# Four row buffers throughout, a later start for part of the first gather, and second products in fp32 in a two-block fp32 network on one core

## The chip, the cores and the metric

The kernel runs on one core of one Trainium2 chip. A core has five engines that run side by side and meet only through semaphores: PE multiplies matrices (PEld in the profile is its weight load), DVE does elementwise work and reductions, ACT does functions and copies with a scale, POOL (GpSimd) does elementwise work too and issues the gathers, SP issues the other transfers. Each engine works through its own list of instructions in order. The metric is the device time of one execution in microseconds (us).

## The reference, cut to what matters

Input `x` has 512 tokens of 1024 numbers, handled as four token tiles of 128. A first block mixes tokens (retention and differential attention), then each token picks 8 times 16 of 16384 single-neuron experts and adds their outputs; a second block (sparse attention, pooling, gates, projections) follows. The picked experts are what this change touches:

```python
ue = jnp.take(u, e, axis=0)      # e: 128 tokens x 8 heads x 16 picks, rows of 1024 floats
ve = jnp.take(v, e, axis=0)
act = jax.nn.gelu(jnp.einsum('thkd,td->thk', ue, xb))
return jnp.einsum('thk,thkd->td', g * act, ve)
```

Everything is float32. `u` and `v` hold 16384 rows of 4 KB, 64 MB each.

## The kernel before, in words

The experts are computed in two ways. **Token tiles 0 and 3 gather** (`gather`, `fetch`): for each of the 128 picks one indirect transfer, issued by POOL, fetches one row of `u` per token into a buffer `rows` of 128x1024 (512 KB). DVE multiplies it with the normalised token and sums (L535). Then 128 fetches from `v`, each multiplied by its weight and added into `gx` (L542). So a tile takes 256 fetches, and the two tiles 512, one tile after the other. `ROWS = 3` buffers `rows` go round: fetch k can be issued when DVE has used fetch k-3. Late in tile 3 one more buffer (`more`) is taken in turn. `issue_after(x)` keeps a fetch behind instruction x in the schedule; `HOLDS` says from which fetch of a tile this x is the end of the spread (`self.mark`, a POOL copy of the last spread column). 256 means never.

**Token tiles 1 and 2 are computed densely** over all 16384 experts, in 128 groups of 128. `up` loads 128 rows of `u` (512 KB), transposes them on PE, multiplies with the 256 tokens and takes the gelu. The first 46 ups multiply in fp32 (`xw`, `EARLY = 36` into `sa`, `WX = 10` more into `w`, "ahead"); the other 82 use three products of a split into two float32r halves (`dh`, with `uT` split by ACT and DVE, L127 and L128). `spread` writes the picks' weights to their expert columns: for 64 groups of four tokens DVE makes two one-hot tiles `E`, ACT scales one (`A`), PE multiplies, DVE multiplies `sa` with the result and DVE or ACT copies the rest into `sb`. `dense` then runs over the 128 groups: load 128 rows of `v`, and four products 128x512 into the sums (`op`, the "down"). With `MIX = (1, 2)` every second down is split: ACT and DVE make halves `h`, `l` of `v` and of the weights, in one buffer each, and PE does three products in float32r in place of one in fp32.

The order on each engine is made when the program is built: a scheduler simulates the program and lists each engine's instructions. Instructions of the gather stand among those of the mixer, of the dense part and of the second block. An engine that stands at a gather instruction whose row has not landed does nothing else.

The stages, by the trace: the mixer and the expert scores of tiles 1 to 3 with tile 0's gather beside them (to about 440 us), early ups and picks (to 724), the spread (724 to 869), the dense part (869 to 1647), the second block of tiles 0 to 2 (from 1647) and of tile 3 (after it). Tile 3's gather ends at about 1850, and its result is needed only by the last of these.

Other names: `scores` normalises a tile into `xnt` (one buffer) and transposes it; `rope_tables` makes sine and cosine tables; L128 on POOL makes the low half `wlo` of a weight.

Of the kernel before, what the change touches and what calls it, by code (L numbers as in the profile page):

```python
# [8 lines left out]
F32 = mybir.dt.float32  # L9
# [57 lines left out]
class Net:  # L67
    def __init__(self, tc, ctx, a, const_at, dbg=None):
        self.tc, self.nc, self.ctx, self.a = tc, tc.nc, ctx, a
        self.dbg = dbg or {}  # L70
        self.const_at = const_at
        nc = self.nc
        pool = lambda name, bufs=1, **k: ctx.enter_context(tc.tile_pool(name=name, bufs=bufs, **k))
        self.keep = pool("keep")
        self.wk = pool("wk", 2)
        self.ps = pool("ps", 1, space=bass.MemoryType.PSUM)
        self.dram = pool("dram", 1, space=bass.MemoryType.DRAM)
        self.ident = self.const(self.keep, "ident")
# [4 lines left out]
        nc.gpsimd.memset(self.half, -0.5)  # L83
        self.turn = 0
        self.whole = True
        self.last = None
# [338 lines left out]
    def scores(self, ts, sp, sw):  # L425

        nc, a, tc = self.nc, self.a, self.tc
        n = len(ts)
        hl = self.pair(n)
        with self.behind():  # L430
            g = self.row(sw, a["norm_ffn_g"], D, "grow", bufs=1)
        for i, t in enumerate(ts):
            xn = sw.tile([P, D], F32, name="xnt", bufs=1)
            self.norm(xn, self.xs[t], g)
            o = DENSE.index(t) * P if t in DENSE else None
            self.tsplit(hl, xn, 0, i, whole=None if o is None else self.xw[:, :, o:o + P])
            if t in GATHER:
                nc.sync.dma_start(self.xnd[t], xn)
            nc.sync.dma_start(self.xd[t], self.xs[t])
        self.normed = self.root.ins  # L440
        for t in ts:
            st = sp.tile([P, 16, P], F32, name=f"s{t}", bufs=1)
            self.s[t] = st
        for b in range(4):
            qT = sw.tile([P, 4, n * P], F32, name="pqT")
            self.projT(hl, a["peer_wq"][0], b * 512, n, qT, [1.0] * 4, sw)
            for i, t in enumerate(ts):
                p = self.sc()
                for j in range(4):
                    nc.tensor.matmul(p[:, j * P:(j + 1) * P], qT[:, j, i * P:(i + 1) * P],  # L450
                                     self.skT[:, 4 * b + j, :], start=True, stop=True)
                nc.scalar.activation(self.s[t][:, 4 * b:4 * b + 4, :].rearrange("p a b -> p (a b)"), p, AF.Copy)
        return hl

    def select(self, t, sw, idx, parts=1):
# [6 lines left out]
        if not dense:  # L462
            ei = self.ga.tile([P, P], I32, name=f"ei{t}", bufs=1)
            gws = self.ga.tile([P, 8, 16], F32, name=f"gw{t}", bufs=1)
            self.ei[t], self.gw[t] = ei, flat(gws)
# [57 lines left out]

    def gather(self, t, hold, more):


        nc, a = self.nc, self.a
        ei, gw = self.ei[t], self.gw[t]
        act = self.ga.tile([P, P], F32, name="act")
        pause = self.normed if t == 0 else None  # L530
        xn = self.ga.tile([P, D], F32, name="gx", bufs=1)
        nc.sync.dma_start(xn, self.xnd[t])
        for k in range(P):
            r = self.fetch(a["peer_u"][0], ei, k, self.mark if k >= hold else pause if k >= PAUSE else None, k >= more)
            nc.vector.scalar_tensor_tensor(r, r, 1.0, xn, op0=OP.mult, op1=OP.mult, accum_out=act[:, k:k + 1])  # L535
# [4 lines left out]
        for k in range(P):  # L540
            r = self.fetch(a["peer_v"][0], ei, k, self.mark if P + k >= hold else pause, P + k >= more)
            nc.vector.scalar_tensor_tensor(x, r, act[:, k:k + 1], x, op0=OP.mult, op1=OP.add)  # L542
# [4 lines left out]

    def fetch(self, src, ei, k, hold, more):
        if more and k % (ROWS + MORE) >= ROWS:
            r = self.gm.tile([P, D], F32, name="more", bufs=MORE)  # L550
        else:
            r = self.ga.tile([P, D], F32, name="rows", bufs=ROWS)
        with self.tc.issue_after(hold) if hold else ExitStack():
# [4 lines left out]
    def spread(self, idx, sa, sb, gb):  # L558
# [3 lines left out]
        full = [P, P, 4]  # L562
        cr = self.const(gb, "row", bufs=1)
        row4 = gb.tile(full, F16, name="row4", bufs=1)
        nc.scalar.activation(row4, cr[:, :, None].to_broadcast(full), AF.Copy)
        for t in range(0, sa.shape[2], 4):
# [50 lines left out]
    def dense(self, ts, hl, sa, sb, dn, ue):  # L617
# [13 lines left out]
        def op(e):  # L631
            v, w = [V.pop(e)], [slot(e)]
            if e % MIX[1] < MIX[0]:
                for x in (v, w):
                    hl_ = [dn.tile(list(x[0].shape), F32R, name=f"{q}{x[0].shape[1]}", bufs=1) for q in "hl"]
                    self.split(*hl_, x[0])
                    x[:] = hl_
# [33 lines left out]

    def rope_tables(self, pool):

# [18 lines left out]
        lim = 3.1415925  # L692
        sin = self.keep.tile(full, F32, name="sin")
        cos = self.keep.tile(full, F32, name="cos")
        nc.vector.tensor_scalar(sin, ang, lim, -lim, op0=OP.min, op1=OP.max)
# [266 lines left out]

ROWS = 3
RAW = 3
HALFE = 4
WX = 10
DEEP = 1
PEB = 2
P0B = 2
VB = 3  # L970
EARLY = 36
MIX = (1, 2)
LASTUP = 124
# [5 lines left out]
HOLD = 252  # L979
HOLDS = [256, 0]  # L980
MORE = 1
MORES = [256, 230]
AB = 3
# [14 lines left out]
def build(tc, a, const_at, dbg=None):  # L998
    with ExitStack() as ctx:
        n = Net(tc, ctx, a, const_at, dbg)  # L1000
        pool = lambda name, bufs=1, **k: tc.tile_pool(name=name, bufs=bufs, **k)
        n.ga = ctx.enter_context(pool("ga", 2, side="right"))
        first(n, pool)
        n.tpn, n.nraw, n.whole, n.lone, n.lo_of = GN, 3, WHOLE, False, LO3
        with pool("tp2") as n.tp, pool("hn2", 2) as n.hn, pool("ws2") as n.ws, pool("b2") as b2, \
                pool("bp") as bp, pool("gm") as n.gm, pool("bw", 2) as bw:
            for t, hold, more in zip(GATHER, HOLDS, MORES):
                n.gather(t, hold, more)
            n.second_setup(b2)
# [3 lines left out]

def first(n, pool):
    n.tpn, n.nraw = 3, 4
    n.whole, n.lone = WHOLE0, True
    nd = len(DENSE) * P
    with ExitStack() as right:
        with pool("xe") as n.xe, pool("tp1") as n.tp, pool("ws1") as n.ws, pool("sk") as sk:
            with pool("b1") as b1, pool("hn") as n.hn:  # L1020
# [10 lines left out]
                n.lo_of = LO2  # L1031
                n.mixer([1, 2, 3])
            n.st = right.enter_context(pool("st", side="right"))
            picks = right.enter_context(ExitStack())
# [56 lines left out]
```

## Time and profile before

| | us |
|---|---|
| three runs | 2151.7, 2159.73, 2160.89 |
| their median | 2159.73 |
| the profiled execution, its own time | 2150.35 |
| its span | 2148.6 |

| engine | busy us | share of the span |
|---|---|---|
| PE | 1870.3 | 87% |
| PEld | 1477.7 | 69% |
| DVE | 1487.0 | 69% |
| ACT | 743.6 | 35% |
| POOL | 822.8 | 38% |

The transfers moved 538 MB, 251 GB/s on the mean. The shares are means over stages that differ: what bounds a stage is read from the windows and waits of that stage. PE's busy time counts modelled ends, so how long a product holds PE is read from the starts of two in a row. A group of fp32 products has two PE instructions for each product of the program.

### The profile page before, as it was taken

The numbers are of one execution on the slowest core, as the hardware profiler recorded it, in microseconds if no ns is written. First come the engines' busy times: TensorE is split into PE (matmuls) and PEld (weight loads), VectorE is DVE, ScalarE is ACT, GpSimd is POOL, SyncE is SP. The second block draws the span as 40 slices with busy tenths as digits, with TensorE's granted clock in tenths as the row PEclk, the third lists the DMA queues.
The fourth block names the chain that finished last, engine by engine and source line by source line (L and its number), as shares of the span: only waits on it lengthen the run. The fifth ranks groups of instructions, "written<-read, shape, count | busy, mean of one in ns | idle before, by whom it ended". The sixth has DMA issues, their size and how long they took to land.

```text
span 2148.6 us, 27755 instructions
## 1 busy us (share of the span) xinstructions
PE 1870.3 (87%) x9646; PEld 1477.7 (69%) x9646; DVE 1487.0 (69%) x3049; ACT 743.6 (35%) x1517; POOL 822.8 (38%) x627
## 2 busy tenths in 40 slices
PE   7798987588898866799999998999996698799998
PEld 6497766488777765577677776777774576677654
DVE  1188787777995799876676666676777789934261
ACT  2243442233433467332232222232232233463231
POOL 0015455443144521443433444333335787433200
PEclk9999999699999899899999999999998789899998
DMA  8847887787458763788899888899897766422872
GB/s 314 288 153 254 274 269 245 269 280 238 145 196 285 263 201 108 249 328 313 314 364 325 312 300 310 324 326 321 316 328 256 241 202 186 132 89 79 287 255 79
DMA packets 182012, 538.23 MB, mean 251 GB/s; under 512 B 18032, under 2 KB 25328, under 8 KB 181744
## 3 DMA queue, kind: packets, MB, share of 16 engines
q0 software_dynamic: 73728, 268.47, 36.4%
q1 hardware_dynamic: 108144, 268.00, 36.0%
q8 instruction: 76, 1.25, 0.2%
q14 instruction: 64, 0.52, 0.1%
HBM read 528.53 MB, written 7.86 MB: 250 GB/s over the span
## 4 chain that ended last, share of the span: by engine, by line
PE 25%; issue 23%; DMA 22%; DVE 18%; POOL 10%; ACT 1%; SPq 0%; POOLq 0%; DVEq 0%; ACTq 0%
DMA rows<-in_peer_v,ei 14%; PE acc L204 12%; POOL rows L554 9%; DMA rows<-in_peer_u,ei 7%; PE acc L232 6%; DVE gx L542 4%; DVE rows L535 2%; PE acc L642 1%; PE tr L153 1%; DVE ix L404 1%; PE sc L924 1%; DVE E L572 1%; PE tr L933 1%; DVE v L402 1%; PE sc L604 1%
## 5 line engine op out<-in xcount | busy, mean ns | idle before, releaser
L554 POOL DMA_INDIRECT rows<-in_peer_u,ei x256 | 313.2, 1224 | 444.6 <-DVE rows L535 344.3
L554 POOL DMA_INDIRECT rows<-in_peer_v,ei x249 | 286.8, 1152 | 426.7 <-DVE gx L542 350.0
L542 DVE SCALAR_TENSOR_TENSOR gx<-rows,act,gx 128x1024 f32<-128x1024 f32 x249 | 349.4, 1403 | 133.3 <-DMA rows<-in_peer_v,ei 128.1
L535 DVE SCALAR_TENSOR_TENSOR rows<-rows,gx 128x1024 f32<-128x1024 f32 x256 | 313.0, 1230 | 181.4 <-DMA rows<-in_peer_u,ei 177.8
L604 PE MATMUL sc<-dh,uT 128*128 128x256 f32 x1968 | 306.7, 305 | 29.2 <-DVE uT L128 17.6
L604 PEld LDWEIGHTS sc<-dh,uT 128*128 128x128 f32 x1968 | 261.9, 195 | 70.0 <-issue 31.3
L204 PE MATMUL acc<-wlo,Thi 128*128 128x512 f32 (+1 forms) x504 | 206.8, 430 | 9.2 <-POOL wlo L128 8.0
L204 PE MATMUL acc<-whi,Thi 128*128 128x512 f32 (+1 forms) x500 | 196.1, 429 | 14.9 <-ACT whi L127 10.6
L604 PE MATMUL sc<-xw,uT 128*128 128x256 f32 x736 | 179.7, 396 | 31.1 <-ACT uT L156 30.1
L128 POOL TENSOR_TENSOR wlo<-raw,whi 128x1024 fp32r<-128x1024 f32 (+1 forms) x62 | 144.7, 2341 | 125.0 <-ACT whi L127 124.5
L204 PE MATMUL acc<-whi,Tlo 128*128 128x512 f32 (+1 forms) x432 | 173.3, 404 | 7.9 <-DVE Tlo L128 7.9
L604 PEld LDWEIGHTS sc<-xw,uT 128*128 128x128 f32 x736 | 141.3, 199 | 52.5 <-ACT uT L156 32.7
L642 PE MATMUL acc<-v,sb 128*128 128x512 f32 x368 | 168.3, 599 | 7.7 <-DVE sb L653 7.7
L127 ACT ACTIVATE whi<-raw 128x1024 fp32r<-128x1024 f32 (+1 forms) x108 | 110.8, 1028 | 149.8 <-PE acc L204 67.1
L605 ACT ACTIVATE w<-sc 128x256 f32<-128x256 f32 x92 | 35.3, 384 | 292.7 <-PE sc L604 290.9
L204 PEld LDWEIGHTS acc<-whi,Thi 128*128 128x128 f32 x500 | 98.8, 200 | 53.0 <-issue 17.1
L204 PEld LDWEIGHTS acc<-wlo,Thi 128*128 128x128 f32 x504 | 101.3, 201 | 45.9 <-issue 18.8
L153 PE MATMUL tr<-c_ident,raw 128*128 128x128 f32 x880 | 131.5, 278 | 1.0 <-PE acc L577 1.0
L127 ACT ACTIVATE uT<-tr 128x512 fp32r<-128x512 f32 x164 | 92.8, 595 | 95.4 <-PE tr L153 84.7
L642 PEld LDWEIGHTS acc<-v,sb 128*128 128x128 f32 x368 | 68.7, 191 | 77.3 <-issue 65.8
L642 PE MATMUL acc<-h,h 128*128 128x512 f32 x256 | 104.4, 416 | 13.3 <-ACT h L127 13.1
L128 DVE TENSOR_TENSOR uT<-tr,uT 128x512 fp32r<-128x512 f32 x164 | 108.4, 685 | 7.5 <-ACT uT L127 7.2
(328 smaller groups left out, 3404.4 us busy)
## 6 DMA issues: line engine op xcount, KB each, us to landing
raw<-in_peer_u SPq DMA_DIRECT2D x128, 512.0 KB, 6.1
v<-in_peer_v SPq DMA_DIRECT2D x128, 512.0 KB, 5.7
raw<-in_w_in SPq DMA_DIRECT2D x79, 512.0 KB, 4.5
raw<-in_w_out SPq DMA_DIRECT2D x22, 512.0 KB, 4.1
whi<-in_w_in SPq DMA_DIRECT2D x21, 512.0 KB, 6.1
raw<-in_peer_wq SPq DMA_DIRECT2D x21, 512.0 KB, 5.9
wlo<-in_w_in SPq DMA_DIRECT2D x20, 512.0 KB, 6.5
rows<-in_peer_u,ei POOLq DMA_INDIRECT x256, 6.5
```

The costliest lines, as they stand in the source:

```text
L127: self.nc.scalar.activation(hi, src, AF.Copy)
L128: (eng or self.nc.vector).tensor_tensor(lo, src, hi.bitcast(F32), OP.subtract)
L153: nc.tensor.transpose(p[:, c, :], src[:, (j + c) * P:(j + c + 1) * P], self.ident)
L204: self.nc.tensor.matmul(ps[i][:, :n], x, y, start=k == 0 and q == 0, stop=k == nk - 1 and q == len(ws) - 1)
L232: nc.tensor.matmul(ps[c][:, :ncol], x, y, start=k == 0 and q == 0, stop=k == 7 and q == len(ws) - 1)
L402: nc.vector.max(v[:, r], src)
L535: nc.vector.scalar_tensor_tensor(r, r, 1.0, xn, op0=OP.mult, op1=OP.mult, accum_out=act[:, k:k + 1])
L542: nc.vector.scalar_tensor_tensor(x, r, act[:, k:k + 1], x, op0=OP.mult, op1=OP.add)
L554: self.nc.gpsimd.indirect_dma_start(out=r, out_offset=None, in_=src, in_offset=bass.IndirectOffsetOnAxis(ap=ei[:, k:k + 1], axis=0))
L604: nc.tensor.matmul(h[:, :nt], x, y, start=f == k == q == 0, stop=f == 1 and k == 3 and q == len(ps) - 1)
L605: nc.scalar.activation(dst, h[:, :nt], AF.Gelu)
L642: mm(o[i][c], x, y, start=e == q == 0, stop=e == P - 1 and q == len(ps) - 1)
```

## The change

- **Rows.** `ROWS` is 4 in place of 3, and the extra buffer `more` is gone.
- **Hold.** `HOLDS` is [168, 0]: fetches of tile 0 from the 169th on stand behind the end of the spread.
- **Downs.** `MIX` is (0, 1): no down is split. The buffers of `v` are 4 in place of 3.
- **Spread.** Of the copies into `sb` 48 of 64 are DVE's and 16 ACT's (32 and 32 before), and its row of constants shares a buffer of `A`.
- **Smaller ones.** `EARLY` 37 and `WX` 9 in place of 36 and 10; two buffers of `xnt`; the sine and cosine tables are made after the scores of tiles 1 to 3, not before those of tile 0; the picks and `act` of the gathers live in pools of their own.

```diff
-            xn = sw.tile([P, D], F32, name="xnt", bufs=1)
+            xn = sw.tile([P, D], F32, name="xnt")
...
-            r = self.fetch(a["peer_u"][0], ei, k, self.mark if k >= hold else pause if k >= PAUSE else None, k >= more)
+            r = self.fetch(a["peer_u"][0], ei, k, self.mark if k >= hold else pause if k >= PAUSE else None)
...
-    def fetch(self, src, ei, k, hold, more):
-        if more and k % (ROWS + MORE) >= ROWS:
-            r = self.gm.tile([P, D], F32, name="more", bufs=MORE)
-        else:
-            r = self.ga.tile([P, D], F32, name="rows", bufs=ROWS)
+    def fetch(self, src, ei, k, hold):
+        r = self.ga.tile([P, D], F32, name="rows", bufs=ROWS)
...
-            if t % 8:
+            if t % 16:
                 nc.vector.tensor_copy(sb[:, :, t:t + 4], g[:, EARLY:, :])
...
-ROWS = 3
+ROWS = 4
-WX = 10
+WX = 9
-VB = 3
-EARLY = 36
-MIX = (1, 2)
+VB = 4
+EARLY = 37
+MIX = (0, 1)
-HOLDS = [256, 0]
-MORE = 1
-MORES = [256, 230]
+HOLDS = [168, 0]
...
-                with pool("rt") as rt:
-                    n.rope_tables(rt)
...
+            with pool("rt") as rt:
+                n.rope_tables(rt, g3)
```

How the instructions move. The first place is POOL's list around the end of the spread, `held`; `oh` belongs to the picks of tile 3, `in_peer_v` before it and behind it is tile 0's gather, `in_peer_u` behind that tile 3's. Before:

```order
L554 DMA rows<-in_peer_v,ei_922 128x1024 x19
L501 TENSOR_TENSOR oh<-oh,ixb 128x2048
L554 DMA rows<-in_peer_v,ei_922 128x1024 x44
L610 COPY held<-sb 128x1
L554 DMA rows<-in_peer_v,ei_922 128x1024 x43
L554 DMA rows<-in_peer_u,ei_4795 128x1024 x26
```

Now:

```order
L501 TENSOR_TENSOR oh<-oh,ixb 128x2048
L555 DMA rows<-in_peer_v,ei_82 128x1024 x8
L501 TENSOR_TENSOR oh<-oh,ixb 128x2048
L613 COPY held<-sb 128x1
L555 DMA rows<-in_peer_v,ei_82 128x1024 x88
L555 DMA rows<-in_peer_u,ei_2800 128x1024 x8
```

Before, 44 fetches stood between the last pick and `held`, and 43 of tile 0 behind it; now none stands between the two, and 88 behind `held`. Up to the point where the second block clears its tail (`MEMSET tail`), 253 fetches stood behind `held` before and 305 do now.

The second place is DVE's list in the dense part, where one up (two `uT`) takes its turn with rows of tile 3. Before:

```order
L653 TENSOR_TENSOR sb<-sb,w 128x256
L535 SCALAR_TENSOR_TENSOR rows,act<-rows,gx 128x1024 x2
L128 TENSOR_TENSOR uT<-tr,uT 128x512 x2
L128 TENSOR_TENSOR l_9344<-sb,h_9343 128x256
L128 TENSOR_TENSOR l_9340<-v,h_9339 128x1024
L535 SCALAR_TENSOR_TENSOR rows,act<-rows,gx 128x1024 x2
```

Now:

```order
L657 TENSOR_TENSOR sb<-sb,w 128x256
L539 SCALAR_TENSOR_TENSOR rows,act_2802<-rows,gx 128x1024
L129 TENSOR_TENSOR uT<-tr,uT 128x512 x2
L539 SCALAR_TENSOR_TENSOR rows,act_2802<-rows,gx 128x1024 x4
L657 TENSOR_TENSOR sb<-sb,w 128x256
```

The halves `l` of the weights and of `v` are gone, and four rows stand in each up's turn where three to four stood.

The third place is the end of tile 3's gather in DVE's list. The names around it are the second block's: `isc` with its MAX and MATCH_REPLACE picks keys, `pe,mx` is softmax, `pfirst` and `uT` pooling. Before:

```order
L542 SCALAR_TENSOR_TENSOR gx<-rows,act,gx 128x1024
L908 MATCH_REPLACE isc<-m_14115,isc 128x384
L908 MATCH_REPLACE isc<-m_14118,isc 128x256
L957 SCALAR_TENSOR_TENSOR uT<-psum__15550,uT 128x384
L371 ISA pe,mx<-sc,c_blk 128x128
L371 ISA mx 128x1
L907 MAX m_14121<-isc 128x8
L907 MAX m_14124<-isc 128x8
L959 COPY uT<-pfirst 128x16
L542 SCALAR_TENSOR_TENSOR gx<-more,act,gx 128x1024
```

Now:

```order
L905 SCALAR_TENSOR_TENSOR isc<-rl,qi,isc 128x256 x2
L546 SCALAR_TENSOR_TENSOR gx<-rows,act_2802,gx 128x1024
L906 TENSOR_TENSOR isc<-isc,c_blk 128x128
L546 SCALAR_TENSOR_TENSOR gx<-rows,act_2802,gx 128x1024
L911 MAX m_13053<-isc 128x8
L912 MATCH_REPLACE isc<-m_13053,isc 128x256
L903 TENSOR_SCALAR isc<-rl,qi 128x384
L905 SCALAR_TENSOR_TENSOR isc<-rl,qi,isc 128x384
L546 SCALAR_TENSOR_TENSOR gx<-rows,act_2802,gx 128x1024
L802 TENSOR_TENSOR qk<-qk,rstd 128x640
L546 SCALAR_TENSOR_TENSOR gx<-rows,act_2802,gx 128x1024
```

The last rows stood among the softmax and the pooling of tiles 0 to 2; now a few more follow the first MAX of the key choice, and none is left when the softmax begins.

## Rows read from the trace of the kernel before

**Rows 1.** Windows by stage: start:end us, length, each engine's busy us, PEclk, DMA share, GB/s.

```profile
440.00:724.00 284.00, 244.98 (x1312) 219.68 (x1312) 230.83 (x770) 98.05 (x170) 113.15 (x81) 0.93 0.67 227
724.00:869.00 145.00, 107.32 (x695) 94.69 (x693) 137.19 (x266) 103.24 (x313) 41.22 (x40) 0.95 0.56 179
869.00:1647.00 778.00, 725.44 (x3896) 559.39 (x3896) 542.42 (x774) 218.43 (x381) 301.38 (x256) 0.98 0.87 315
1647.00:1850.00 203.00, 143.81 (x627) 114.44 (x626) 173.96 (x237) 62.70 (x112) 146.84 (x94) 0.82 0.65 207
1850.00:2149.00 299.00, 285.38 (x1185) 191.39 (x1183) 122.05 (x298) 113.81 (x209) 68.74 (x32) 0.97 0.47 156
```

**Rows 2.** Waits of PE, 869 to 1647: waiting line, releaser, total us, times, longest.

```profile
PE sc L604 <- DVE uT L128: 17.6, 12, 3.1
PE acc L642 <- ACT h L127: 13.1, 10, 2.9
PE sc L604 <- ACT dh L127: 8.2, 1, 8.2
...
PE acc L642 <- DVE l L128: 4.3, 5, 1.1
```

**Rows 3.** Waits of DVE, 869 to 1647.

```profile
DVE rows L535 <- DMA rows<-in_peer_u,ei: 104.3, 39, 5.0
```

**Rows 4.** Windows, POOL instructions on `rows` (fetches) alone: busy us, (count), clock, DMA, GB/s.

```profile
869.00:1647.00 778.00, 296.45 (x253) 0.98 0.87 315
```

**Rows 5.** DMA issues by line, 869 to 1647: count, KB each, median us to landing.

```profile
rows<-in_peer_u,ei POOLq DMA_INDIRECT x128, 7.0
```

**Rows 6.** DMA issues by line, 790 to 868.

```profile
rows<-in_peer_v,ei POOLq DMA_INDIRECT x16, 4.3
```

**Rows 7.** DMA view, 880 to 1000: rate in 40 slices of 3 us.

```profile
GB/s 339 400 333 303 164 276 377 386 251 333 374 369 389 332 403 367 344 188 156 419 421 235 247 393 404 369 385 362 126 329 399 309 182 304 358 348 89 411 412 320
```

**Rows 8.** Waits of PE, 1647 to 1850.

```profile
PE sc L924 <- DVE mx L371: 18.3, 2, 11.2
```

**Rows 9.** Timeline of DVE, 1769 to 1850: start us, length, line, operation.

```profile
1769.85 0.43 DVE L907 MAX8 m<-isc 128x8 f32<-128x256 f32 x1
...
1848.94 1.27 DVE L542 SCALAR_TENSOR_TENSOR gx<-more,act,gx 128x1024 f32<-128x1024 f32 x1
```

**Rows 10.** Timeline of PE, 1207.6 to 1222 (merged where alike).

```profile
1207.84 0.40 PE L642 MATMUL acc<-h,l 128*128 128x512 f32 x1
...
1210.13 3.59 PE L642 MATMUL acc<-v,sb 128*128 128x512 f32 x8
...
1215.79 2.65 PE L604 MATMUL sc<-dh,uT 128*128 128x256 f32 x20 [1.60 <-DVE uT L128]
1218.28 1.04 PE L153 MATMUL tr<-c_ident,raw 128*128 128x128 f32 x8
1219.07 0.48 PE L642 MATMUL acc<-h,h 128*128 128x512 f32 x1
```

**Rows 11.** Timeline of PE's weight loads (PEld), 1213.3 to 1214.

```profile
1213.56 0.42 PEld L604 LDWEIGHTS sc<-dh,uT 128*128 128x128 f32 x3 [0.24 <-issue]
```

**Rows 12.** Windows, DVE instructions on `rows` alone, in the spread.

```profile
724.00:869.00 145.00, 51.04 (x40) 0.95 0.56 179
```

**Rows 13.** Groups of DVE instructions in the spread: count, busy us, mean ns, idle before.

```profile
L582 DVE COPY sb<-acc 128x368 f32<-128x368 f32 x32 | 17.7, 552 | 0.0
```

**Rows 14.** Groups of ACT instructions in the spread.

```profile
L584 ACT ACTIVATE sb<-acc 128x368 f32<-128x368 f32 x32 | 14.8, 462 | 19.9 <-DVE sa L580 19.8
```

**Rows 15.** Waits of PE in the spread, 724 to 869.

```profile
PE acc L577 <- DVE E L572: 21.6, 27, 1.6
```

**Rows 16.** Waits of PE, 165 to 440.

```profile
PE tr L153 <- DVE xnt L145: 22.8, 3, 12.4
```

**Rows 17.** Waits of PE, 440 to 724.

```profile
PE sc L604 <- ACT uT L156: 28.5, 7, 11.3
```

**Rows 18.** Timeline of ACT, 0 to 1: an activation table load.

```profile
0.72 1.28 ACT L255 ACT_TABLE_LOAD   x1 [0.72 <-PEq L1077]
```

More of the change, by code (lines that the diff above doesn't have):

```diff
@@ L83, in __init__ @@
         nc.gpsimd.memset(self.half, -0.5)
+        self.picks, self.act = {}, {}
         self.turn = 0
@@ L462, in select @@
         if not dense:
-            ei = self.ga.tile([P, P], I32, name=f"ei{t}", bufs=1)
-            gws = self.ga.tile([P, 8, 16], F32, name=f"gw{t}", bufs=1)
+            ei, gws = self.picks[t]
             self.ei[t], self.gw[t] = ei, flat(gws)
@@ L522, in select, with room, gather @@
             nc.scalar.activation(self.gk[:, o:o + P], p[:, 2, :], AF.Copy)
-    def gather(self, t, hold, more):
+    def room(self, t, pool):
+        self.picks[t] = pool.tile([P, P], I32, name=f"ei{t}"), pool.tile([P, 8, 16], F32, name=f"gw{t}")
+        self.act[t] = pool.tile([P, P], F32, name=f"act{t}")
+    def gather(self, t, hold):
         nc, a = self.nc, self.a
         ei, gw = self.ei[t], self.gw[t]
-        act = self.ga.tile([P, P], F32, name="act")
+        act = self.act[t]
         pause = self.normed if t == 0 else None
@@ L540, in gather @@
         for k in range(P):
-            r = self.fetch(a["peer_v"][0], ei, k, self.mark if P + k >= hold else pause, P + k >= more)
+            r = self.fetch(a["peer_v"][0], ei, k, self.mark if P + k >= hold else pause)
             nc.vector.scalar_tensor_tensor(x, r, act[:, k:k + 1], x, op0=OP.mult, op1=OP.add)
@@ L562, in spread @@
         full = [P, P, 4]
-        cr = self.const(gb, "row", bufs=1)
+        cr = gb.tile([P, 4, P], F32, name="A", bufs=AB)[:, 0, :]
+        o, _ = self.const_at["row"]
+        nc.sync.dma_start(cr, self.a["consts"][:, o:o + P])
         row4 = gb.tile(full, F16, name="row4", bufs=1)
@@ L634, in op @@
                 for x in (v, w):
-                    hl_ = [dn.tile(list(x[0].shape), F32R, name=f"{q}{x[0].shape[1]}", bufs=1) for q in "hl"]
+                    hl_ = [dn.tile(list(x[0].shape), F32R, name=f"h{x[0].shape[1]}", bufs=1),
+                           dn.tile(list(x[0].shape), F32R, name=f"l{x[0].shape[1]}", bufs=1)]
                     self.split(*hl_, x[0])
@@ L669, in after, with rope_tables @@
         return x
-    def rope_tables(self, pool):
+    def rope_tables(self, pool, keep):
         nc, a = self.nc, self.a
@@ L692, in rope_tables @@
         lim = 3.1415925
-        sin = self.keep.tile(full, F32, name="sin")
-        cos = self.keep.tile(full, F32, name="cos")
+        sin = keep.tile(full, F32, name="sin")
+        cos = keep.tile(full, F32, name="cos")
         nc.vector.tensor_scalar(sin, ang, lim, -lim, op0=OP.min, op1=OP.max)
@@ L1002, in build @@
         n.ga = ctx.enter_context(pool("ga", 2, side="right"))
-        first(n, pool)
+        n.room(0, ctx.enter_context(pool("g0", side="right")))
+        first(n, pool, ctx)
         n.tpn, n.nraw, n.whole, n.lone, n.lo_of = GN, 3, WHOLE, False, LO3
         with pool("tp2") as n.tp, pool("hn2", 2) as n.hn, pool("ws2") as n.ws, pool("b2") as b2, \
-                pool("bp") as bp, pool("gm") as n.gm, pool("bw", 2) as bw:
-            for t, hold, more in zip(GATHER, HOLDS, MORES):
-                n.gather(t, hold, more)
+                pool("bp") as bp, pool("bw", 2) as bw:
+            for t, hold in zip(GATHER, HOLDS):
+                n.gather(t, hold)
             n.second_setup(b2)
@@ L1011, in build, with first @@
                 n.second(ts, bp, bw)
-def first(n, pool):
+def first(n, pool, ctx):
     n.tpn, n.nraw = 3, 4
@@ L1032, in first @@
                 n.mixer([1, 2, 3])
+            g3 = ctx.enter_context(pool("g3", side="right"))
+            n.room(3, g3)
             n.st = right.enter_context(pool("st", side="right"))
```

## The prediction

> **What bounds the kernel now.** I read the windows by stage first, then the waits inside each stage, then the timeline where a wait needed a price. The windows [rows 1] show no single bound. In the spread (145 us) DVE works 137.2 us: DVE bounds it. In the dense part (778 us) PE works 725 us with modelled ends, and its waits [rows 2] name the other engines for little: 17.6 us on DVE's `uT`, 13.1 on ACT's `h`, 8.2 at the start on `dh`, 4.3 on `l`. DVE itself stands there 104 us waiting for `u` rows alone [rows 3], and a `uT` queued behind such a row is late. The transfers run at 315 GB/s with 253 fetches issued [rows 1, 4]: one fetch each 778/253 = 3.07 us, so with three buffers a round of 9.2 us, of which 7.0 us pass from issue to landing [rows 5]. At 109 GB/s in the spread's later part the landing takes 4.3 us [rows 6]. From 1647 to 1850 PE works only 144 of 203 us, at a mean granted clock of 0.82 between its levels of 1.2 and 2.4 GHz, with stands before it; its longest wait is 18.3 us on softmax maxima from DVE [rows 8], whose list is filled with rows until 1849 [rows 9]. After that PE works 285 of 299 us: it bounds the end, and tile 3's gather is not waited for but stands in others' way.
>
> **Early stages.** The norm of the next tile no longer waits for the last one's transposes, since `xnt` has two buffers. PE waits for `xnt` 22.8 us in three waits, the first of 12.4 [rows 16]; the first stays, the other two (10.4) mostly go: -8. One fp32 up more stands ahead of the spread. By the timeline's spacing of 0.43 us for an fp32 product of 512 columns [rows 10, 11] its 16 instructions of 256 columns take half of that each, with eight transposes of 0.10 us: 16 x 0.215 + 0.8 = 4.2, say +4. Four more table loads of 1.28 us [rows 18] come where PE already waits 28.5 us for ACT's `uT` [rows 17]: 0 to +5, taken as +4 with the 13 short DVE operations of the tables. Fetches of tile 0 come faster with four buffers; that can shorten DVE's stands or slow weight loads, which I cannot sign. Sum 0, with -25 (all the `xnt` wait and some more) and +15 (none of it, and both additions doubled) as ends.
>
> **The spread.** By 724, when it begins, about as many fetches have been issued as the new limit of 168 allows, so nothing is lost before it. Behind the held fetch POOL has only fetches, 88 of tile 0 and the first of tile 3, so the wait stops nobody else; DVE's list has their rows behind the spread too. The 40 rows inside it, 51.0 us of DVE [rows 12], go behind it. Added on DVE are 16 copies of 0.55 us less about 0.1 that overlaps, +7.2 [rows 13]: 137.2 - 51.0 + 7.2 = 93. ACT drops 16 copies of 0.46 [rows 14] and one up's evacuations (1.6): 103.2 - 7.4 - 1.6 = 94. PE drops one up: 107.3 - 5 = 102. So the stage cannot go below 102 (-43); if PE's wait of 21.6 us on `E` [rows 15] and half as much on ACT stay on top of it, it is 135 (-10). I take 110, nearer to the busiest engine since the wait on `E` was DVE being full: -35.
>
> **The dense part.** The 64 split downs become fp32. Products in float32r start 0.229 us apart (1207.84 to 1210.13, ten of them), a down has 12: 2.75 us. The fp32 down starts at 1210.13, and the load behind the first following one at 1213.56: 3.43 us for 8 [rows 10, 11]. That is +0.69 on PE, times 64 = +44. (The eight seem to end at 1213.16, but the next product's start there is followed by a gap; the weight loads show the true pace.) Going by an up of 24 x 0.1245 + 0.79 = 3.8 us [rows 10] and 82 of them, PE's floor was 176 + 220 + 310 + 10 (`dh`) = 716 of the 778; it becomes 440 + 310 + 10 = 760. The stalls were 62. The waits for `h` and `l`, 17.4, go with the splits, which leaves 45. Also gone are 64 splits of `v` and of the weights on ACT and DVE; a down then waits for the landing of `v` alone, three groups ahead with four buffers, which I cost at nothing. How much of the rest goes depends on the rows. DVE's list has 305 - 253 = 52 fetches more in this stage, and they must come at 788/305 = 2.58 us, a round of 10.3 us for four buffers against 9.2 now. That leaves 1.1 us for slower landings. The bytes: 315 GB/s x 778 = 245 MB, plus 52 x 0.524 = 272 MB, in 788 us 346 GB/s. On a line through 4.3 us at 109 GB/s and 7.0 at 315 the landing grows to 7.4, by 0.4. So rows come early enough more often than before, and I take 28 of the 45 us as staying: 788, +10. Ends: no stall, 760 (-18); all 45, 805 (+27).
>
> The Trainium skill (FP8 and Floating Point Precision, TensorE Precision Notes) counts four passes for true fp32. With the float32r spacing for each pass that would be 4 x 0.229 = 0.92 us in place of the 0.86 that the rows show, and an estimate of +59 us in place of +44; the rows decide.
>
> **The second block.** Rows left for it by the lists are 39 in place of 46, and the last one stands where the first key choice does, which ran at 1769.85; before it was at 1848.94 [rows 9]. Softmax of tiles 0 to 2 then meets no gather on DVE, nor POOL's issues between weight splits. The 18.3 us wait goes, and a little of the slow clock with it: -20. Ends: -45 (three quarters of the 59 us that PE does not work before 1850) and 0 (the rows that crowd into its first 120 us take back what the later part gives).
>
> **Sum.** 0 - 35 + 10 - 20 = -45. Against the profiled execution's 2150.35 that is 2105. The median of the three runs is 9.4 above that execution and the lowest 1.4 above; I add 3: 2108.
>
> **Rivals.** *Transfers at their limit (slower).* If the transfers cannot go past 315 GB/s, 272 MB take 865 us, the fourth row only waits longer in the queue, and rows that stand ahead of `uT` in DVE's list hold PE: dense +87 in place of +10, so 2108 + 77 = 2185. It decides from a dense part of 833 us on (no gain in all), 2.73 us for a fetch or 327 GB/s. For it: landings already take 7.0 against 4.3 us. Against it: slices of 3 us reach 421 GB/s, and 369 to 403 are common [rows 7]. The Trainium skill (DMA: Bandwidth & Descriptors, Specifications) gives a core about 358 GB/s of its memory; the slices pass that for short, and by that limit, as an estimate, 272 MB would take 761 us, and this rival would not decide.
>
> *The gains are covered (no change).* In the spread the engines wait on each other in turn (-10), in the dense part all 45 us of stalls stay (+27), and the second block gives 5: +12, so 2165. For it: each wait in [rows 2] is short and spread over several engines, as in a chain without one bound.
>
> *More than forecast.* Two rows more in hand take nearly all stalls from the dense part (-10), early stages give 12, the spread reaches its floor (-43), the second block 35: -100, so 2053. For it: DVE's list loses all splits `l`, and its stands on rows are long [rows 3].
>
> That the hold does nothing would need fetch 169 to come late anyway; the 40 rows inside the spread [rows 12] speak against it.
>
> **How the numbers follow.** The forecast has 0.64 (its own range 2075 to 2140), the larger gain 0.13, no change 0.12, the transfer limit 0.11. About 0.5% (11 us) is what a measurement of this kernel can tell: faster means below 2149, slower above 2170. Faster: 0.62 of the forecast, the larger gain 0.13 and 0.02 of no change, 0.77. Same: 0.02 and 0.07, 0.09. Slower: the transfer limit and 0.03, 0.14. The range of 8 in 10 is 2052 to 2158: it reaches to the larger gain and part of the way to no change, and leaves out the transfer limit.
>
> **What would show it.** Right: a spread of about 110 us without L542 in it, a dense part of 770 to 805 us with DVE's waits for `u` rows under the 104 us of now, some 340 GB/s in it, and the gather's end within 140 us of the dense part's. Wrong: PE's wait for `uT` grown and the landing of rows past 8.1 us (the transfer limit); a spread over 125 us; softmax waiting as long as before; or fp32 downs further apart than 0.43 us.

## The result and the profile after

The changed kernel takes 2058.9 us (median of four runs, 2055.9 to 2063.5) against 2160.3 for the kernel before beside it: ratio 0.9535, 95% interval 0.9498 to 0.9573. I had forecast 2108, with 2052 to 2158 as the range. The side was right and the gain was twice the forecast: 101 us in place of 52. The profiled execution has a span of 2055.5 us, 93 less than before.

The windows of the changed kernel, cut at its own stages (columns as in [rows 1]: start:end us, length, busy us of PE, PEld, DVE, ACT and POOL with their instructions, PEclk, DMA share, GB/s):

```profile
165.00:414.00 249.00, 214.22 (x1058) 176.19 (x1057) 217.32 (x414) 96.77 (x205) 158.10 (x117) 0.92 0.88 306
414.00:662.00 248.00, 230.54 (x1287) 209.51 (x1286) 216.40 (x768) 103.63 (x175) 114.77 (x70) 0.97 0.69 235
662.00:786.00 124.00, 107.76 (x740) 95.87 (x738) 99.62 (x244) 100.59 (x302) 0.00 (x0) 1.00 0.14 48
786.00:1569.00 783.00, 761.69 (x3640) 504.08 (x3640) 516.26 (x693) 124.25 (x252) 363.04 (x309) 0.99 0.95 347
1569.00:1700.00 131.00, 86.83 (x387) 70.01 (x387) 103.31 (x117) 36.09 (x62) 103.92 (x70) 0.82 0.78 255
1700.00:2056.00 356.00, 337.91 (x1423) 232.28 (x1422) 170.42 (x414) 140.61 (x259) 102.15 (x48) 0.97 0.46 146
```

Four stages are followed through all kernels below: early (up to the first one-hot of the spread), spread (up to DVE's last product into `sa`), dense (up to PE's last down), second block. The row counts are how many of the gather's 512 rows DVE works off in each stage, counted from the trace; the "gather end" is DVE's last row against the dense part's end.

| kernel | early | spread | dense | second | span | rows by stage | gather end |
|---|---|---|---|---|---|---|---|
| before | 724.1 | 144.0 | 779.4 | 501.1 | 2148.6 | 172 / 38 / 253 / 49 | +203 |
| after | 662.3 | 123.3 | 783.1 | 486.8 | 2055.5 | 168 / 0 / 302 / 42 | +132 |
| difference | -61.8 | -20.7 | +3.7 | -14.3 | -93.1 | | |
| forecast | 0 | -35 | +10 | -20 | -45 | | |

So one term carries the surprise: the early stages, which I had put at nothing. Waits of DVE for rows in them, before (165 to 724) and after (165 to 662); the columns are the waiting line, the releaser, total us, times, longest:

```profile
DVE rows L535 <- DMA rows<-in_peer_u,ei: 73.5, 56, 4.9
DVE gx L542 <- DMA rows<-in_peer_v,ei: 30.2, 22, 3.2
```

```profile
DVE rows L539 <- DMA rows<-in_peer_u,ei: 37.6, 34, 3.5
DVE gx L546 <- DMA rows<-in_peer_v,ei: 7.1, 7, 1.9
```

104 us of stands become 45, and what is queued behind rows on DVE comes earlier. On PE's side 20 of the 62 us are its own busy time: 465 us before (220.3 in the first line below and 245.0 in the second stage of [rows 1]) and 445 after (6.5 us of the difference are work put off, as the account of the prediction says), at a mean granted clock of 0.91 before and 0.95 after. The other 42 us are time in which it stood.

```profile
165.00:440.00 275.00, 220.30 (x1067) 180.07 (x1066) 211.84 (x394) 97.01 (x208) 137.90 (x111) 0.89 0.80 266
```

PE's waits in the same stretch after (165 to 662) answer to [rows 16, 17]: 9.5 in place of 22.8 us for `xnt`, 11.5 in place of 28.5 for ACT's `uT`.

```profile
PE sc L607 <- ACT uT L157: 11.5, 4, 3.7
PE tr L154 <- DVE xnt L146: 9.5, 1, 9.5
```

In the dense part PE now works 762 of 783 us by modelled ends. More than half of its waits (786 to 1569), 11.5 us, are at the start, on `dh`; compare [rows 2]:

```profile
PE sc L607 <- ACT dh L128: 6.1, 1, 6.1
PE acc L646 <- DVE sb L657: 6.1, 9, 3.1
PE sc L607 <- DVE dh L129: 5.4, 1, 5.4
PE sc L607 <- ACT uT L128: 2.1, 7, 0.4
```

DVE has changed places with PE there. Its longest wait is now for what PE's ups release, and the stands on `u` rows fell from 104.3 [rows 3] to 32.4 us:

```profile
DVE sb L657 <- ACT w L608: 136.1, 68, 8.7
DVE gx L546 <- DMA rows<-in_peer_v,ei: 76.4, 78, 2.8
DVE rows L539 <- DMA rows<-in_peer_u,ei: 32.4, 45, 2.3
```

The fetches from issue to landing, in the same stretch (count, KB, median us), against 7.0 in [rows 5]:

```profile
rows<-in_peer_v,ei POOLq DMA_INDIRECT x177, 7.3
rows<-in_peer_u,ei POOLq DMA_INDIRECT x128, 7.4
```

Two stretches of PE's timeline after (start us, length, line, operation, count) give the price of the fp32 downs: from 819.76 to 830.37 two downs, one up and its transposes take 10.61 us. My prices make 2 x 3.43 + 3.8 = 10.66.

```profile
819.76 7.03 PE L646 MATMUL acc<-v,sa 128*128 128x512 f32 x16
826.23 3.43 PE L607 MATMUL sc<-dh,uT 128*128 128x256 f32 x24
829.50 1.04 PE L154 MATMUL tr<-c_ident,raw 128*128 128x128 f32 x8
830.37 7.03 PE L646 MATMUL acc<-v,sa 128*128 128x512 f32 x16
```

Modelled ends hide one more wait. In the later half of the dense part PE takes one down, one up and eight transposes in turn. In the changed kernel a turn takes 7.50 us, since the first weight load of its down waits for DVE's `sb`; without the hold (a kernel of the experiments) it takes 7.17 us. First PE's timeline of one turn (start us, length) and the weight load at its end, in the changed kernel; then a turn without the hold; then the waits of the weight loads (PEld), in the same order, 786 to 1569 and 824 to 1595.

```profile
1272.73 3.70 PE L646 MATMUL acc<-v,sb 128*128 128x512 f32 x8
1280.23 3.70 PE L646 MATMUL acc<-v,sb 128*128 128x512 f32 x8
1280.22 0.30 PEld L646 LDWEIGHTS acc<-v,sb 128*128 128x128 f32 x2 [0.29 <-DVE sb L657]
```

```profile
1311.21 3.60 PE L646 MATMUL acc<-v,sb 128*128 128x512 f32 x8
1318.38 3.60 PE L646 MATMUL acc<-v,sb 128*128 128x512 f32 x8
```

```profile
PEld acc L646 <- DVE sb L657: 18.3, 43, 3.3
```

```profile
PEld acc L646 <- DVE sb L657: 11.1, 15, 2.3
```

Counted from the traces, 34 turns of the changed kernel take 7.4 to 7.6 us and 2 take 7.1 to 7.3; without the hold these are 5 and 34. So some 9 us of the dense part come from where `sb` is made in the order of the instructions.

In the second block (waits of PE, 1569 to 2055) the softmax's wait of 18.3 us [rows 8] is down to 4.9, but others stand in its place while the last 42 rows go through DVE:

```profile
PE tr L154 <- DVE h L146: 14.5, 2, 10.9
PE acc L205 <- ACT whi L128: 12.5, 1, 12.5
PE acc L205 <- POOL wlo L129: 10.2, 9, 2.0
PE sc L928 <- DVE mx L372: 4.9, 2, 4.5
```

### The profile page after: what moved, and what is told of

It reads as the page before. It is cut to its first block, busy times and chain, and to the rows that moved or that the text cites. A ratio compares the mean times of both kernels' runs of the same rounds, so it can differ in the third digit from the quotient of the medians.

```text
span 2055.5 us, 26830 instructions
## 1 busy us (share of the span) xinstructions
PE 1881.2 (92%) x9390; PEld 1404.6 (68%) x9390; DVE 1387.6 (68%) x2936; ACT 651.3 (32%) x1377; POOL 855.6 (42%) x627
## 4 chain that ended last, share of the span: by engine, by line
PE 33%; issue 17%; DMA 15%; DVE 15%; POOL 9%; ACT 2%; POOLq 0%; DVEq 0%; ACTq 0%
PE acc L205 10%; POOL rows L555 8%; PE acc L646 8%; DMA rows<-in_peer_v,ei 8%; PE sc L607 7%; DMA rows<-in_peer_u,ei 6%; PE tr L154 2%; DVE rows L539 2%; DVE gx L546 2%; PE acc L233 1%; DVE ix L405 1%; PE sc L928 1%; ACT A L578 1%; DVE v L403 1%; PE tr L937 1%
## 5 line engine op out<-in xcount | busy, mean ns | idle before, releaser
L555 POOL DMA_INDIRECT rows<-in_peer_u,ei x256 | 323.8, 1265 | 319.7 <-DVE rows L539 226.7
L555 POOL DMA_INDIRECT rows<-in_peer_v,ei x256 | 318.0, 1242 | 318.4 <-DVE gx L546 200.9
L646 PE MATMUL acc<-v,sb 128*128 128x512 f32 x728 | 329.3, 598 | 8.2 <-DVE sb L657 6.1
L607 PE MATMUL sc<-dh,uT 128*128 128x256 f32 x1968 | 295.0, 304 | 13.5 <-ACT dh L128 6.1
L607 PEld LDWEIGHTS sc<-dh,uT 128*128 128x128 f32 x1968 | 252.1, 192 | 61.1 <-issue 44.5
L646 PEld LDWEIGHTS acc<-v,sb 128*128 128x128 f32 x728 | 132.4, 190 | 157.2 <-issue 138.7
L607 PE MATMUL sc<-xw,uT 128*128 128x256 f32 x736 | 173.0, 386 | 11.5 <-ACT uT L157 11.5
L646 PE MATMUL acc<-v,sa 128*128 128x512 f32 x296 | 130.8, 592 | 0.0
L657 DVE TENSOR_TENSOR sb<-sb,w 128x256 f32<-128x256 f32 x82 | 34.8, 425 | 136.1 <-ACT w L608 136.1
L154 PE MATMUL tr<-c_ident,raw 128*128 128x128 f32 x880 | 120.2, 272 | 0.0
```

The source lines that it names most:

```text
L154: nc.tensor.transpose(p[:, c, :], src[:, (j + c) * P:(j + c + 1) * P], self.ident)
L555: self.nc.gpsimd.indirect_dma_start(out=r, out_offset=None, in_=src, in_offset=bass.IndirectOffsetOnAxis(ap=ei[:, k:k + 1], axis=0))
L607: nc.tensor.matmul(h[:, :nt], x, y, start=f == k == q == 0, stop=f == 1 and k == 3 and q == len(ps) - 1)
L646: mm(o[i][c], x, y, start=e == q == 0, stop=e == P - 1 and q == len(ps) - 1)
L657: nc.vector.tensor_tensor(slot(done), slot(done), self.early(done, hl, nt, dn, 1, ue, HALFE), OP.mult)
```

## The experiments

Two theories on the early stages. Theory 1: the fourth row buffer shortens DVE's stands on rows. Theory 2: the small edits (two `xnt` buffers, the rope tables' place, the order that follows) gave it. A third question came up with the results: what the hold is worth. Every kernel was timed beside the kernel before on the same chip; ratios are to that.

**Three rows again.**

```diff
-ROWS = 4
+ROWS = 3
```

> The changed kernel with three row buffers in place of four, all else as it is. Theory 1 (the fourth buffer keeps DVE from standing on rows of the gather, so what is queued behind them in its list comes earlier): in the early stages DVE's waits for rows go back from 45 us towards the 104 us of the kernel before, the spread starts at 700 to 725 us in place of 662, and the whole takes 2110 to 2170 us. Theory 2 (the 62 us of the early stages come from the smaller edits: two buffers of xnt, the rope tables' place, the order that follows from them): the spread still starts at 660 to 680 us, and only the dense part and the second block lose something, 2065 to 2095 us.

Measured 2164.0 us, ratio 1.0037 (1.0012 to 1.0063): the whole gain is gone. Stages 709.4 / 123.7 / 822.1 / 508.3, rows 166 / 2 / 288 / 56. DVE's stands in the early stages are back (first fence, 165 to 709), and in the dense part PE waits for `uT` and `sb` behind rows (second fence, 834 to 1655):

```profile
DVE rows L539 <- DMA rows<-in_peer_u,ei: 73.7, 56, 3.6
DVE gx L546 <- DMA rows<-in_peer_v,ei: 26.6, 17, 4.9
```

```profile
PE acc L646 <- DVE sb L657: 27.7, 24, 3.1
PE sc L607 <- DVE uT L129: 16.4, 10, 3.6
```

Theory 1 holds: with all the other edits in place the fourth buffer is worth 47 us in the early stages, 39 in the dense part and 22 in the second block. Of the 44 us of waits in the second fence, DVE spends 30 on rows or waiting for them. Against the kernel before, this run's early stages are 15 us shorter (709.4 for 724.1): so much do all the other edits give there without the fourth buffer.

**One `xnt` buffer again.**

```diff
-            xn = sw.tile([P, D], F32, name="xnt")
+            xn = sw.tile([P, D], F32, name="xnt", bufs=1)
```

> The changed kernel with one xnt buffer, as before the change. Theory 1 (the fourth row buffer gave the early stages): the up-products' start moves from 414 us to at most 424 (the two later waits of PE for xnt, 10.4 us in the kernel before, come back), the rest keeps its length, 2059 to 2070 us. Theory 2 (the second xnt buffer frees DVE's list and with it the whole early part): the spread starts at 690 to 725 us, 2085 to 2125 us.

2092.3 us, ratio 0.9723 (0.9665 to 0.9782). Stages 688.7 / 119.5 / 789.0 / 491.7. PE's waits for `xnt` come back at their old size (165 to 689):

```profile
PE tr L154 <- DVE xnt L146: 21.7, 3, 10.8
```

That is 12 us more than after, and the spread still starts 26 us later, with DVE's waits for rows almost as short (52 us). The mark at 414 us (the first transposes of `raw` behind the mixer) moves to 423, as theory 1 says, but the total lies in the range of theory 2, and the start of the spread 1 us ahead of it. So the second `xnt` buffer has a share, and it is more than the wait that I had priced at 8; by what way the rest comes is not shown.

**Two `xnt` buffers on the kernel before** (the same line the other way).

> The kernel before with two buffers of xnt, all else as before. Theory 1 (the second xnt buffer is worth the 20 to 35 us that its loss cost the changed kernel, independent of the row buffers): the spread starts at 690 to 705 us in place of 724, 2125 to 2140 us. Theory 2 (its worth comes with the fourth row buffer, since DVE's list stands on rows anyway): the up-products start some 8 us earlier and the spread starts at 710 to 720 us, 2145 to 2157 us.

2162.4 us, ratio 1.0032 (1.0004 to 1.006): nothing won. Stages 714.1 / 140.3 / 783.0 / 518.4, rows 170 / 36 / 253 / 53. The spread starts 10 us earlier, as the `xnt` wait says (9.1 us in one time), but the gather ends at 1862 us in place of 1850, and the second block takes the gain back. So theory 2 has it as far as the spread's start, and the total is 5 us above even its range: alone this edit buys nothing, while with the fourth row buffer it is worth 26 us early and 33 in all.

**No hold.**

```diff
-HOLDS = [168, 0]
+HOLDS = [256, 0]
```

> The changed kernel without the hold: no fetch waits for the end of the spread. Theory of the prediction: the spread takes 20 to 35 us more than its 124, since rows stand on DVE in it again, the dense part gets fewer rows and is within 10 us of its 782, the second block does not change: 2065 to 2090 us. Rival (the rows only change places, and what the spread saves the dense part pays): 2050 to 2065 us, no difference that a measurement can tell.

2038.1 us, ratio 0.9470 (0.9414 to 0.9526): faster than the changed kernel by some 21 us between the medians (14 by the ratios; the runs of the two do not overlap), below both expectations. Stages 680.3 / 143.4 / 771.3 / 439.8, rows 180 / 36 / 296 / 0; the gather ends 5 us ahead of the dense part's end. The hold therefore gives 18 us early and 20 in the spread, and costs 12 in the dense part and 47 in the second block: +21. Of the 18 us 7 are work put off into the spread: before the spread begins, 593 fp32 products of ups have been issued with the hold and 626 without it, 0.216 us each. Of the 12 us some 9 are the longer turns shown above. In the windows of the second block without the hold, PE works 141 of the first 155 us at a granted clock of 0.97; in the changed kernel it is 87 of 131 us at 0.82:

```profile
1595.00:1750.00 155.00, 140.65 (x669) 109.97 (x670) 110.96 (x257) 70.47 (x136) 85.32 (x50) 0.97 0.39 120
1750.00:2035.00 285.00, 271.74 (x1141) 180.82 (x1139) 103.41 (x227) 104.46 (x186) 64.81 (x30) 0.99 0.48 159
```

**The hold alone on the kernel before.**

```diff
-HOLDS = [256, 0]
+HOLDS = [168, 0]
```

> The kernel before with the hold alone: fetches from the 169th on wait for the end of the spread, three row buffers, split downs. Theory 1 (the hold moves the 40 rows of the spread to the end of the gather, where a row costs more than inside the spread): the spread takes 120 to 125 us in place of 145, the dense part 775 to 790, the gather ends 280 to 330 us behind it in place of 203, and the second block takes 515 to 540 us in place of 501, 2150 to 2180 us in all. Rival (theory of the prediction: most of what the spread saves is kept): 2120 to 2145 us.

2140.3 us, ratio 0.9923 (0.9897 to 0.9948). Stages 725.2 / 116.3 / 778.4 / 520.5, rows 168 / 0 / 251 / 93, the gather's end 348 us behind the dense part. The total lies in the rival's range, my own step, but not for its reason: 28 us come out of the spread and 19 go into the second block, as theory 1 has it, so that 8 are left between the two profiled spans and 16 between the medians. Here the gather ran far into the second block anyway, so 44 rows more there cost 0.44 us each. In the changed kernel the hold is what pushes it there at all.

**The hold released at the spread's start.**

```diff
-HOLD = 252
+HOLD = 0
```

> The changed kernel with the hold released by the first group of the spread in place of the last: fetches from the 169th on wait until the spread begins. Theory 1 (a row costs by its place: the 14 that the kernel without the hold puts ahead of the spread cost it 18 us, the 38 inside the spread 20 us, and a row that is left for the second block more than 1 us): the spread starts at 660 to 668 us, takes 140 to 146 us, the gather ends 20 to 45 us behind the dense part, 2020 to 2040 us in all. Rival (only that the gather ends with the dense part counts, so the hold costs whatever it pushes past it): the second block takes 455 to 470 us in place of the 440 without the hold, 2040 to 2055 us.

2047.1 us, ratio 0.9487 (0.9430 to 0.9544). Stages 657.1 / 151.4 / 791.5 / 447.0, rows 168 / 36 / 304 / 4. The total falls to the rival, the stages to neither: the early gain is there (-23 against no hold), but the spread takes 8 us more and the dense part 20. The spread holds the same 33 products more than without the hold (143 for 110), which is 7 of its 8 us. In the dense part 33 turns take 7.4 to 7.6 us here and 5 without the hold, which is some 8 of the 20 us; the rest stays open.

**All downs in fp32 on the kernel before.**

```diff
-MIX = (1, 2)
+MIX = (0, 1)
```

> The kernel before with all downs in fp32, all else as before (three rows with the one more near the end, three buffers of v, no hold). Theory of the prediction (PE's own work in the dense part grows by 44 us, and its short waits take up only a part of it): the dense part goes from 778 to 785 to 810 us, and the whole takes 2160 to 2185 us. Rival (the splits on DVE and ACT cost as much as they save on PE, because rows and uT stand behind them): the dense part is 765 to 780 us, the whole 2140 to 2160 us.

2158.4 us, ratio 1.0014 (0.9990 to 1.0039). Stages 724.4 / 144.4 / 818.2 / 473.0, rows 172 / 38 / 277 / 25. The dense part grows by 39 us, past the end that theory 1 gave it; yet the total lies in the rival's range, since 24 more rows are worked off in the longer dense part and the second block is 28 us shorter for it. So the price on PE is as theory 1 has it, or above, and the total was missed for want of the second block. PE's waits there (870 to 1687) are for `uT` and `sb`, as with three rows above. Together they are 17.5 us longer than before (7.7 for `sb` there), as much as the waits for `h` and `l` (17.4) that went with the splits:

```profile
PE sc L604 <- DVE uT L128: 31.4, 20, 2.6
PE acc L642 <- DVE sb L653: 11.4, 14, 2.1
```

**Three buffers of `v`.**

```diff
-VB = 4
+VB = 3
```

> The changed kernel with three buffers of v in place of four. Theory of the prediction (the fourth buffer of v is worth nothing while v is asked for three groups ahead): the dense part within 4 us of its 782, 2056 to 2064 us. Rival (an fp32 down keeps v longer, since there is no split that frees it, and PE waits for v's landing): the dense part takes 795 to 830 us, PE's waits for v show, 2070 to 2110 us.

2057.8 us, ratio 0.9529 (0.9472 to 0.9586): no difference from the changed kernel, the dense part 779.8. The fourth buffer of `v` is worth nothing, as costed.

**Fewer rows in the dense part.**

```diff
-        for k in range(P):
+        for k in range(P if t == 0 else 0):
             r = self.fetch(a["peer_v"][0], ei, k, self.mark if P + k >= hold else pause)
```

> The changed kernel without the 128 v rows of tile 3 (the last part of the second gather is left out), so that some 216 rows stand in the dense part in place of 302 and none behind it; TensorE's work is the same. Theory 1 (the dense part is at TensorE's own work, 760 us as the prediction worked it out, and the 22 us above it come from rows and their transfers): the dense part takes 757 to 767 us, the second block 435 to 450, 1985 to 2005 us in all. Rival (the 22 us are hand-offs between engines that have nothing to do with rows): the dense part takes 776 to 786 us, 2005 to 2020 us in all.

2004.7 us, ratio 0.9300 (0.9274 to 0.9327). Stages 662.2 / 123.3 / 776.8 / 441.2, rows 168 / 0 / 216 / 0. With 86 rows fewer the dense part shortens by 6 us only, and PE is as busy in it as in the changed kernel (window 786 to 1562):

```profile
786.00:1562.00 776.00, 761.80 (x3640) 504.77 (x3640) 410.90 (x608) 125.59 (x253) 251.90 (x219) 0.99 0.79 291
```

The dense part is the rival's; the total lies where the two ranges meet (2005). Nor do the 216 rows that remain slow PE where they can be compared: in two stretches of this run, the first with rows and the second with none left, PE starts as many instructions in 60 us (321 and 320).

```profile
1266.00:1326.00 60.00, 59.46 (x321) 42.26 (x321) 42.10 (x72) 11.67 (x25) 26.69 (x24) 1.00 0.97 349
1386.00:1446.00 60.00, 59.55 (x320) 42.35 (x320) 13.71 (x24) 11.72 (x25) 0.00 (x0) 1.00 0.39 140
```

So with four buffers the rows are hidden under PE in the dense part. The long turns are here too (46 of 7.4 to 7.6 us, some 15 us over turns of 7.17). The second block without a row takes 441 us, as without the hold.

**32 of the spread's copies on ACT**, without the hold.

```diff
-            if t % 16:
+            if t % 8:
```

> The changed kernel without the hold, and with every second group's last copy of the spread on ACT again, as before the change (8 copies of 0.55 us more taken from DVE than now). Theory 1 (with rows in the spread DVE bounds it): the spread takes 137 to 141 us in place of 144.5, 2030 to 2036 us. Rival (engines wait for each other in turn, so a copy moved to ACT only moves the wait): 143 to 147 us, 2035 to 2042 us.

2033.1 us, ratio 0.9429 (0.9373 to 0.9485), the fastest kernel that was run with all the work in it: its interval lies below the changed kernel's, but overlaps that of the kernel without the hold alone. The spread is 139.4, inside theory 1's range, but the expectation miscounts: the edit moves 16 copies to ACT (from 16 to 32), 8.8 us of DVE, not 8. By theory 1 that would be about 135; 4 of the 8.8 us came, so the other half went as the rival has it.

**48 of them on ACT**, without the hold.

```diff
-            if t % 16:
+            if t % 16 == 0:
```

> The changed kernel without the hold, and with 48 of the spread's 64 last copies on ACT in place of 16 (32 of 0.55 us taken from DVE, 32 of 0.46 us put on ACT). With rows in it the spread took 144.5 us at 16 on ACT and 140.1 at 32. Theory 1 (DVE bounds it): 128 to 136 us, 2020 to 2032 us in all. Rival (ACT takes DVE's place as the bound, since it has the scaled one-hots to write as well): 138 to 150 us, 2031 to 2045 us.

2038.4 us, ratio 0.9455 (0.9431 to 0.9479). The spread falls to 134.1, inside theory 1 and again by about half of the 17.6 us taken from DVE, but the dense part is 779.5 against 771.3, and the total is the rival's. DVE works 130.5 of 134 us there (fence: window 680 to 814). The 8 us that came back in the dense part go with the order there: 38 turns take 7.4 to 7.6 us in place of 5.

```profile
680.00:814.00 134.00, 105.78 (x685) 93.37 (x684) 130.53 (x251) 107.93 (x327) 46.90 (x40) 0.97 0.59 197
```

**Almost no gather before the spread.**

```diff
-HOLDS = [168, 0]
+HOLDS = [2, 0]
```

> The changed kernel with the hold from the third fetch on, so that all but two rows of the gather come behind the spread. Theory 1 (rows that stand in DVE's list are what still lengthens the early stages: 168 of 1.27 us, and 45 us of waits for their landing): the spread starts at 590 to 630 us in place of 662, the spread itself and the dense part keep their length (124 and 778 to 790 us), and the 166 rows pushed behind the dense part cost the second block some 0.4 to 1.1 us each, 2080 to 2170 us in all. Rival (with four buffers the rows fill gaps of DVE in the early stages and cost nothing there): the spread starts at 650 to 662 us, 2120 to 2200 us in all.

2239.2 us, ratio 1.0377 (1.0350 to 1.0403). Stages 606.4 / 123.3 / 770.4 / 742.7, rows 2 / 0 / 298 / 212. The early stages are as theory 1 has them, 56 us shorter without 166 rows, with PE busy 421 of 441 us (first row). The total misses its range: in the second block (second row) PE works 451 of 742 us at a clock of 0.78, and one of its waits, for the `h` of the tile that the gather has not finished, is 188 us long (waits of PE, 1500 to 2242, in the fence behind the windows).

```profile
165.00:606.00 441.00, 420.74 (x2339) 372.91 (x2338) 241.40 (x886) 196.14 (x374) 42.30 (x20) 0.98 0.32 107
1500.00:2242.00 742.00, 450.76 (x1809) 319.02 (x1808) 532.52 (x784) 182.04 (x326) 417.20 (x289) 0.78 0.71 236
```

```profile
PE tr L154 <- DVE h L146: 199.2, 3, 188.3
```

Set together, four-buffer kernels give a price for a row by its place: 56 us / 166 = 0.34 us in the early stages taken whole ((18 - 7) / 12 = 0.9 for the last twelve of them, by the run without the hold, less the work put off), 20 / 36 = 0.56 in the spread, 47 / 42 = 1.1 to 303 / 212 = 1.4 in the second block (the latter with the wait for the gather's own end in it; the hold alone on the kernel before has 0.44). In the dense part no price shows: 770 us with 298 rows, 777 with 216, 783 with 302.

## Why the prediction was right in direction and short in size

**Early stages, the mis-sized term: 0 forecast, -62 measured.** The step that failed is the sentence that faster fetches "can shorten DVE's stands or slow weight loads, which I cannot sign". I priced what the change does to PE's named waits (`xnt`, -8) and its additions (+8), and gave the fourth buffer no value ahead of the dense part, though it acts wherever DVE stands on a row, and the trace of before had 104 us of such stands there. The runs show 47 us for the buffer in place of 0, with the other edits in place, and 15 for the other edits without it (10 for the second `xnt` buffer alone): 62, outside the ends of -25 and +15 that the term had. Taken from the changed kernel, the second `xnt` buffer costs 26 in place of 8, so its worth depends on the fourth row buffer. The order moved too: before the spread begins, the changed kernel has issued 593 fp32 products of ups, the one before 623, so about 30 x 0.216 = 6.5 us of the 62 are work put off into the spread.

**The spread: -35 forecast, -21 measured.** The rows left it as forecast, and PE's waits fell from 21.6 us on `E` [rows 15] and 11.3 on `A` to 15.1 on `E` and ACT's `A` together. But I had taken 110 us, near the busiest engine, and it is 123: PE works 107, where I had 102, for the 6.5 us put off stand here, DVE works 100, and DVE waits 15.2 us for PE's `acc` (waits of PE, then of DVE, 662 to 786):

```profile
PE acc L580 <- ACT A L578: 8.8, 19, 0.5
PE acc L580 <- DVE E L575: 6.3, 13, 0.8
```

```profile
DVE sa L583 <- PE acc L580: 15.2, 12, 3.5
```

They take turns, as the rival of covered gains had it. The hold alone gave -28, and with 32 copies on ACT the spread was 116. The copies put on DVE cost, as the step with 16 of them back on ACT shows (-4 without the hold).

**The dense part: +10 forecast, +4 measured.** The price of the downs and the rate held, but the number is near by luck: two misses cancel. I had +44 on PE less 17 for the waits that go with the splits, +27, and took 17 of it back with the fourth buffer. Three-buffer kernels with fp32 downs grew by 39 and 43 us, since as long waits for `uT` and `sb` came in place of those for `h` and `l`, and the fourth buffer took 39 of it back. What stays above 760 is 23 us where I took 28, and rows do not show as its cause: the pace is the same with none left. Some 9 of it are the longer turns, for which no term stood in the working. 347 GB/s against 346, and landings of 7.3 to 7.4 us against 7.4, came as worked out, so the rival of a transfer limit did not occur. The Trainium skill (FP8 and Floating Point Precision, TensorE Precision Notes) has four passes for fp32, by which the estimate was +59. The trace has 2 x 0.429 = 0.858 us for an fp32 product of 512 columns and 0.229 for one in float32r, 3.75 times as long: the count is near, and the estimate somewhat high. The Trainium skill (DMA: Bandwidth & Descriptors, Specifications) gives about 358 GB/s for a core. The 347 of the whole stage stay below it, while slices of 20 us in it reach 404, so this run does not show it as a limit.

**The second block: -20 forecast, -14 measured.** The softmax wait fell from 18.3 to 4.9 us, near what was said, but others took its place. What I did not ask is what the block would take with no row in it: 440 us, 47 below. By ending the gather 132 us into it, the hold costs more than it gives, and I had credited it with gains alone. It was a part of the sum with the wrong sign: -93 in span came with the hold, -114 without it.

**The total.** 2058.9 lies in the range of 2052 to 2158 near the end that the rival *More than forecast* (2053, a chance of 0.13) set. That rival's terms did not come: it had 12 early, 10 in the dense part, 43 in the spread and 35 in the second block. So that the range holds the result is luck as far as the mechanism goes.

**Not tried:** the fourth row buffer alone on the kernel before, so that its worth is known with the other edits only; nor the tables' place, `EARLY` and `WX` by themselves.

## What to carry to other kernels

Where an in-order engine works off fetched rows between other jobs, add up its stands on them over the whole span before pricing a further buffer: the worth lies in what is queued behind, in stages where nothing seems to bind. A wait that clears one stage of such rows must be priced at the stage where they end up, and by whether the chain of fetches still ends under work that hides it. Price a row by its place: here 0 us in the PE-bound part, 0.3 in the early stages, 0.6 in the DVE-bound spread, over 1 where it delays the last block of the four-buffer kernels. Look at the waits of weight loads too: modelled ends of PE can hide them.

## What the runs showed of the hardware

- Transfers held 347 GB/s over 783 us with the DMA engines 95% busy, while the landing of an indirect fetch of 512 KB stayed at 7.3 to 7.4 us. At 315 GB/s it was 7.0.
- The granted clock was 1.00 in the spread without rows (15 us of PE's waits for `E` and `A`) and 0.90 to 0.97 with rows in it. The total of these waits does not order it: 0.95 at 33 us (before), 0.90 at 31 (no hold), 0.97 at 25 (48 copies on ACT). It was 0.87 in the first 54 us of the dense part, where PE stands 11.5 us for `dh`.
- The same 3640 products of the dense part kept PE busy for 753 to 767 us in the kernels with fp32 downs. A part of it are waits of the weight loads for `sb`, which modelled ends count as busy: 753 to 754 us in the three kernels with 9 to 17 such waits (no hold, 32 copies on ACT, almost no gather before the spread), 762 in three with 43 to 47 (the changed kernel, fewer rows, 48 copies on ACT), 758 in one with 31 (three buffers of `v`). The 766 to 767 of four others, the two with three row buffers among them, are not explained.
